# A decoder block on one core: early reloads, a regrouped Toeplitz product, and PSUM dealt from one pool

## The chip, the cores and the metric

The kernel runs on one core of a Trainium2 chip. Its time is the device time of one execution in microseconds. The median of three runs is given; lower is better. TensorE (PE) does the matrix products; VectorE (DVE), ScalarE (ACT) and GpSimd (POOL) do the elementwise work; SyncE (SP) mostly issues DMAs, of which POOL also issues some.

## The reference

One layer, 512 positions, width 1024, all float32. With h = RMSNorm(x), one projection h @ w_in gives eight pieces: u_s, z_s, q, k, v, z_a, r_s, r_a. Then

```
y_s = s5_branch(u_s, ...)                        # diagonal complex state space, 64 groups of 16 channels, 64 states
y_s = (y_s * silu(z_s)) @ w_ssm_out
q, k = rope(rms_norm(q)), rope(rms_norm(k))      # 3 dilated groups x 8 heads x 64
y_a = dilated_attention(q, k, v)
y_a = (y_a * silu(z_a)) @ w_attn_out
m   = sigmoid(r_s) * y_s + sigmoid(r_a) * y_a
out = x + m @ w_o

s5_branch(u):   h[l] = ab * h[l-1] + bb @ u[l]   # complex, per group
                y[l] = Re(c @ h[l]) + d_skip * u[l]
                g = gelu(y);  return g * sigmoid(g @ w_glu)
```

## The kernel before, in words

**Projections.** Each float32 operand is split into two rounded halves, hi and lo, and a product becomes three matmuls (hi·hi, lo·hi, hi·lo; `mm3`, all recorded at L63; transposes at L67). `hT_hi` and `hT_lo` hold h transposed. `cm_unit` takes one 1024x128 piece of weights and issues 24 matmuls of 512 columns into a PSUM tile `pj`. Weights come in the order of a list, two pieces ahead: `load_w` sends the DMA on SP's queue (L189) into one of two buffers `w_raw`, ACT rounds it to `w_hi` (L108), and DVE subtracts to get `w_lo` (L110). A third load into `w_raw` can only start when both readers of the first are done.

**S5 branch.** Positions are taken in chunks of eight. There are eight units j, each of eight groups (128 channels).

- `u_unit(j)`: a projection, copied by ACT into `uT` (L286), written by SP to a DRAM buffer `ud[j]` (L287). Later it is read back in another layout by `load_u` (L266), into a tile `Uj` from the pool of small buffers `t2k`.
- `w_unit(j)`: coefficients of chunk input to chunk state, by `coef` (L277 to L279: a product, a second product, a sum, each 128x512, twice per unit), then eight transposes into two PSUM tiles `wps`, copied by ACT into `W` (L299). The first product and the sum run on DVE; the second product runs on the engine that `coef` is given.
- `x_unit(j)`: `load_u`, then 16 matmuls into `xps`, copied by ACT into the chunk states `Xs`.
- A scan over chunks on DVE, L614 to L665, reads and writes `Xs`.
- `ca_unit(j)`: loads C, turns it by matmuls with an identity into `cps`, negates parts into `p3`, and runs `coef` (each op 128x576) for the coefficients `ca` of chunk state to output.
- `m_unit(j)`: 16 matmuls `kps` with `ca` give the in-chunk (Toeplitz) products, 16 rows by 128 columns each. A product reads one of two halves of the rows of the array (h) and writes one of four column groups (a = a0 + h). ACT copies them to `kt` (four copies, L734), POOL adds the skip term (L735), and POOL sends eight DMAs (L739) that lay `kt` out as a block Toeplitz matrix `M`, in one of three buffers.
- `y_unit(j)`: 16 matmuls with `M` and the reloaded u, then 32 with `ca` and `Xs`, into two tiles `yps`, copied to `ysb` (L765). `g_unit(j)` transposes it into `yT`, and ACT (L776) and DVE apply gelu and split it into `gT`.

Between these steps the program places other projections, called fillers (gates z_a and z_s, values, r_s, r_a), to keep PE busy. After the branch come w_glu, w_ssm_out, then attention for four pairs of heads (`qtp`: q and k turned and split at L873 on ACT and L874 on DVE; `sps`: scores; `ptp` and `ot`: probabilities turned, and values), w_attn_out and w_o.

**PSUM.** Eight banks: a pool `ps_p` of three buffers for `pj` and a pool `ps_g` of five for the rest. Behind the S5 branch these are closed and replaced by pools of four, three and one (`ot`). Each pool hands out a buffer as one comes free.

**Order.** Each engine has its own list of instructions, in an order fixed when the program is built: a scheduler of the framework moves instructions by its own estimates of when their operands and buffers are ready. So a change in one place moves instructions on all engines.

Of the kernel before, what the change touches and what calls it, by code (L numbers as in the profile page):

```python
# [11 lines left out]
F32 = mybir.dt.float32  # L12
# [8 lines left out]
P = 128  # L21
D = 1024
S = 512
# [29 lines left out]
def tile_hybrid_block(ctx: ExitStack, tc: tile.TileContext, x, positions, norm_w, w_in, lam_re, lam_im,  # L53
# [24 lines left out]
    tmp = ctx.enter_context(tc.tile_pool(name="tmp", bufs=6))  # L78
    sml = ctx.enter_context(tc.tile_pool(name="sml", bufs=2))
    dram = ctx.enter_context(tc.tile_pool(name="dram", bufs=1, space=DRAM))  # L80
    ps_first = ExitStack()
    ps_p = ps_first.enter_context(tc.tile_pool(name="ps_p", bufs=3, space=PSUM))
    ps_g = ps_first.enter_context(tc.tile_pool(name="ps_g", bufs=5, space=PSUM))

    scr_t = big.tile([P, 4096], F32, name="scr", tag="s4")
    scr_o = [0]
# [11 lines left out]
        return v if dtype == F32 else v.bitcast(dtype)  # L98

    def bank(name):  # L100
        return ps_g.tile([P, 512], F32, name=name, tag="g")

    def t2k(name, dtype=F32):
        return tmp.tile([P, 512], dtype, name=name, tag="t2k")
# [89 lines left out]

    def cm_unit(rh, rl, kts=KT):
        hi, lo = get_w()
        ps = ps_p.tile([P, 512], F32, name="pj", tag="pj")
        for k in range(kts):
            mm3(ps, hi[:, k], lo[:, k], rh[:, k], rl[:, k], k == 0, k == kts - 1)
        return ps  # L200
# [62 lines left out]
    def load_u(j, Uj=None):  # L263
        if Uj is None:
            Uj = t2k("Uj")
        sp.dma_start(Uj, ud[j].rearrange("q g s c -> s q g c"))  # L266
        return Uj.rearrange("p (g c) -> p g c", g=8)
# [21 lines left out]
    def w_unit(j):  # L289
        ba = ab[j % 2][:, 0:8 * T * Q].rearrange("p (a g k q) -> p a g k q", a=2, g=4, k=T)  # L290
        p4 = slice(4 * j, 4 * j + 4)
        for a in range(2):
            coef(ba[:, a], 4 * j, BB[:, 1 + a, p4], BB[:, a, p4], 1, T + 1, ab[2][:, 512 * a:], pool)
        W = big.tile([P, 8, P], F32, name="W", tag=("s6a", "s6b")[j % 2])
        for h in range(2):
            ps = bank("wps")
            for g in range(4):
                pe.transpose(ps[:, g * P:(g + 1) * P], ba[:, h, g].rearrange("p k q -> p (k q)"), ident)
            act.copy(W[:, 4 * h:4 * h + 4].rearrange("p g n -> p (g n)"), ps)  # L299
        return W  # L300

    def x_unit(j, W):
        Uj = load_u(j)
        ps = bank("xps")
        pv = ps.rearrange("p (a g c) -> p a g c", a=2, g=4)
        for g in range(4):
            for a in range(2):
                for h in range(2):
                    pe.matmul(pv[64 * h:64 * h + 64, a, g, :], W[:, 4 * a + g, 64 * h:64 * h + 64], Uj[:, 2 * g + h, :],
                              start=True, stop=True, skip_group_check=True)  # L310
        for a in range(2):
            act.copy(Xsv[:, a, 4 * j:4 * j + 4, NJ:C], pv[:, a, :, 0:C - NJ])
            act.copy(Xsv[:, a, 4 * j:4 * j + 4, 0:NJ], pv[:, a, :, C - NJ:C])

    first = [(get_w(), ps_p.tile([P, 512], F32, name="pj", tag="pj")) for _ in range(3)]
    for h in range(2):
        for (hi, lo), ps in first:
            for k in range(KT):
# [144 lines left out]

    for j in range(3, 8):
        u_unit(j)
        wx(*((), (), (0,), (1,), (2, 3))[j - 3])


    sza = cst.tile([P, NP, S], F32, name="sza")
    gd = dram.tile([2, KT, P, S], F32, name="gd")  # L470

    def gate_tile():
# [95 lines left out]

    def tok_granule():

        pss = [ps_p.tile([P, 512], F32, name="pj", tag="pj") for _ in range(2)]
        for kh in range(2):
            hi, lo = get_w()
            for b in range(2):
                for rr in range(2):
                    r = 2 * b + rr
                    o = pss[b][:, rr * 256:(rr + 1) * 256]
                    for k in range(4):
                        kk = 4 * kh + k
                        mm3(o, hT_hi[:, kk, r * P:(r + 1) * P], hT_lo[:, kk, r * P:(r + 1) * P],  # L580
                            hi[:, k], lo[:, k], kh == 0 and k == 0 and rr == 0, kh == 1 and k == 3)
        return pss
# [109 lines left out]
    def ca_unit(j):  # L692

        cn = sml.tile([P, P], F32, name="cn")
        rows = slice(j * P, (j + 1) * P)
        sp.dma_start(cn[:, 0:64], c_re[0].rearrange("g p n -> (g p) n")[rows])
        sp.dma_start(cn[:, 64:128], c_im[0].rearrange("g p n -> (g p) n")[rows])
        ps = bank("cps")
        for i in range(3):
            a = i % 2  # L700
            for h in range(2):
                pe.matmul(ps[64 * h:64 * h + 64, 64 * i:64 * i + 64], cn[:, 64 * a:64 * a + 64], idp[:, h],
                          start=True, stop=True, skip_group_check=True)

        p3 = sml.tile([P, 3, 4, Q], F32, name="p3")
        p3f = p3.rearrange("p a g q -> p (a g q)")
        act.copy(p3f[:, 0:64], ps[:, 0:64])
        act.activation(p3f[:, 64:192], ps[:, 64:192], AF.Copy, scale=-1.0)
        ca = ab[j % 3].rearrange("p (a g k q) -> p a g k q", a=2, g=4, k=9)
        for a in range(2):  # L710
            coef(ca[:, a], 4 * j, p3[:, a], p3[:, a + 1], 0, 9, abt[:, 3 * nca:], dve)

        dg = sml.tile([Q, 8, Q], F32, name="dg")
        sp.dma_start(dg.rearrange("q g p -> q (g p)"), d_skip[0:1, rows].to_broadcast([Q, P]))
        pool.tensor_tensor(dg, dg, ident[0:Q, 0:Q].unsqueeze(1).broadcast_to([Q, 8, Q]), op=ALU.mult)
        return ca, dg

    def m_unit(j, ca, dg):

        kt = big.tile([Q, 8, T, Q], F32, name="kt", tag=("s7a", "s7b")[j % 2])  # L720
        ps = bank("kps")

        for a0 in (0, 2):
            for b in range(2):
                for c in range(2):
                    for h in range(2):
                        a, m = a0 + h, 2 * b + a0 // 2
                        sl = slice(64 * h, 64 * h + 64)
                        pe.matmul(ps[32 * a:32 * a + Q, b * P:(b + 1) * P], BB[sl, 1 + c, 4 * j + m, :],
                                  ca[sl, c, m, 1:9, :], start=c == 0, stop=c == 1, skip_group_check=True,  # L730
                                  tile_position=(64 * h, 32 * a))
        kv = kt.rearrange("q (b a) k p -> q a b (k p)", a=4)
        for a in range(4):
            act.copy(kv[:, a], ps[32 * a:32 * a + Q, 0:2 * P].rearrange("q (b m) -> q b m", b=2))  # L734
        pool.tensor_tensor(kt[:, :, T - 1, :], kt[:, :, T - 1, :], dg, op=ALU.add)  # L735

        M = Mb[j % 3]
        for t in range(T):
            pool.dma_start(M[Q * t:Q * t + Q, :, 0:P - Q * t], kt[:, :, t:].rearrange("q g k p -> q g (k p)"))  # L739
        return M  # L740
# [75 lines left out]

    def wide_granule(th, tl, mid=None):

        pss = [ps_p.tile([P, 512], F32, name="pj", tag="pj") for _ in range(NB)]
        for kq in range(4):  # L820
            if mid:
                mid(kq)
            hi, lo = get_w()
            for r in range(NB):
                for k in range(2):
                    kk = 2 * kq + k
                    mm3(pss[r], th[:, kk, r * P:(r + 1) * P], tl[:, kk, r * P:(r + 1) * P], hi[:, k], lo[:, k],
                        kk == 0, kk == KT - 1)
        return pss
# [156 lines left out]
        return Pt  # L986

    def values(hp, Pt, V):
        ot = ps_o.tile([P, 512], F32, name="ot", tag="o")
        ov = ot.rearrange("d (r b j) -> d b r j", r=4, b=4)  # L990
        pend = []

# [44 lines left out]
        split(aT[:, 0, hp], aT[:, 1, hp], at, lo_eng=pool)  # L1037


    ps_first.close()  # L1040
    ps_p = ctx.enter_context(tc.tile_pool(name="ps_p2", bufs=4, space=PSUM))
    ps_g = ctx.enter_context(tc.tile_pool(name="ps_g2", bufs=3, space=PSUM))
    ps_o = ctx.enter_context(tc.tile_pool(name="ps_o", bufs=1, space=PSUM))
    yT_hi = big.tile([P, KT, S], F32R, name="yT_hi", tag="s1")
    yT_lo = big.tile([P, KT, S], F32R, name="yT_lo", tag="s2")
    for c in range(KT):
# [81 lines left out]
    for cc in range(KT // 2):  # L1128
        hi, lo = get_w()
        for c2 in range(2):  # L1130
            c = 2 * cc + c2
            if c in rals:
                th = rals[c]
            else:
                th = t2k("ral")
                sp.dma_start(th, rad[c])
            ps = ps_p.tile([P, 512], F32, name="pj", tag="pj")
            for k in range(NP):
                mm3(ps, hi[:, k, c2 * P:(c2 + 1) * P], lo[:, k, c2 * P:(c2 + 1) * P], aT[:, 0, k], aT[:, 1, k],
                    k == 0, k == NP - 1)  # L1140
            dve.scalar_tensor_tensor(th, th, 1.0, ps, op0=ALU.add, op1=ALU.mult)
            dve.tensor_tensor(th, th, m1[:, c], op=ALU.add)
            split(mT_hi[:, c], mT_lo[:, c], th, scale=0.5)
# [38 lines left out]
```

## Time and profile before

| what | value |
|---|---|
| three runs | 727.94, 728.95, 730.92 us, median 728.95 |
| profiled execution | 727.79 us, of which the profile's span is 726.0 and 1.8 lie around it |
| PE busy | 691.6 us, 95% of the span, 4821 matmuls |
| DVE, ACT, POOL busy | 455.4, 314.6, 190.9 us |
| mean granted clock of PE | 0.991 |
| S5 branch: first W coefficients to the last gelu | about 57 to 282 us of the span |

A busy time adds up one engine's instructions; what the program waits for is read from the idle time of PE and from what ended it. Times inside the trace are in us from the start of the span. A matmul of 512 columns is listed with 0.39 us, but the next one starts before its end, so prices of matmuls are taken from the starts of a row of them.

### The profile page before, as it was taken

How to read it: one execution, taken by the hardware profiler on the slowest of the kernel's cores; microseconds unless marked ns; L12 is line 12 of the kernel's file. 1: busy time of each engine (PE TensorE's matmuls, PEld its weight loads, DVE VectorE, ACT ScalarE, POOL GpSimd, SP SyncE). 2: the span in 40 equal slices, each digit the busy share in tenths (PEclk: the TensorE clock that was granted, in tenths of full speed). 3: DMA queues.
4: the chain of work that ended last, by engine and by line, in shares of the span. 5: the costliest groups of instructions: out<-in, count | busy, mean ns of one | idle time of the engine just before them, and what ended most of it. 6: DMA issues, size and time to landing. Idle time of an engine off the chain costs nothing.

```text
span 726.0 us, 12680 instructions
## 1 busy us (share of the span) xinstructions
PE 691.6 (95%) x4821; PEld 574.3 (79%) x4821; DVE 455.4 (63%) x912; ACT 314.6 (43%) x631; POOL 190.9 (26%) x346
## 2 busy tenths in 40 slices
PE   2799799999999999999999999999989998999997
PEld 2787687788978887888889888788868877888886
DVE  6859663999956645764325659755764667464832
ACT  6433453332326465442144456537253725443320
POOL 3426540140205343450000326121601160230000
PEclk9999899999999999999999999999999999999999
DMA  8433652564546544455333432322312231327441
GB/s 206 106 99 93 169 135 79 142 159 132 122 131 147 127 105 138 129 166 185 95 102 94 131 88 63 84 59 59 115 32 60 62 112 30 116 74 249 130 145 58
DMA packets 137213, 82.14 MB, mean 113 GB/s; under 512 B 32696, under 2 KB 125632, under 8 KB 137024
## 3 DMA queue, kind: packets, MB, share of 16 engines
q1 hardware_dynamic: 135088, 78.96, 38.0%
q0 software_dynamic: 2048, 2.36, 2.6%
q8 instruction: 38, 0.62, 0.4%
q14 instruction: 23, 0.19, 0.1%
q10 hardware_dynamic: 16, 0.00, 0.0%
HBM read 68.46 MB, written 10.49 MB: 109 GB/s over the span
## 4 chain that ended last, share of the span: by engine, by line
PE 89%; DVE 3%; ACT 2%; SPq 2%; DMA 2%; issue 1%; ACTq 0%
PE pj L63 73%; PE sps L63 3%; PE yps L63 3%; PE ot L63 2%; PE ptp L67 2%; PE kps L63 2%; PE xps L63 1%; DMA Uj<-ud 1%; PE qtp L67 1%; SPq L443 1%; PE wps L67 1%; DVE w_lo L110 1%; DMA w_raw<-in_w_in_dram 1%; ACT qkp L873 1%; SPq L219 1%; ACT w_hi L108 1%
## 5 line engine op out<-in xcount | busy, mean ns | idle before, releaser
L108 ACT ACTIVATE w_hi<-w_raw 128x1024 fp32r<-128x1024 f32 x100 | 106.1, 1062 | 231.8 <-PE pj L63 197.4
L110 DVE TENSOR_TENSOR w_lo<-w_raw,w_hi 128x1024 fp32r<-128x1024 f32 x98 | 124.5, 1271 | 106.5 <-ACT w_hi L108 106.0
L63 PE MATMUL pj<-hT_lo,w_hi 128*128 128x512 f32 (+1 forms) x344 | 130.9, 381 | 3.6 <-DVE hT_lo L252 3.6
L63 PE MATMUL pj<-hT_hi,w_hi 128*128 128x512 f32 (+1 forms) x344 | 130.8, 383 | 2.0 <-ACT V L905 1.4
L63 PE MATMUL pj<-hT_hi,w_lo 128*128 128x512 f32 (+1 forms) x344 | 130.7, 381 | 1.6 <-DVE w_lo L110 1.6
L63 PE MATMUL pj<-w_hi,hT_hi 128*128 128x512 f32 (+1 forms) x288 | 105.6, 368 | 0.0
L63 PE MATMUL pj<-w_lo,hT_hi 128*128 128x512 f32 (+1 forms) x288 | 105.6, 367 | 0.0
L63 PE MATMUL pj<-w_hi,hT_lo 128*128 128x512 f32 (+1 forms) x288 | 105.2, 368 | 0.0
L63 PEld LDWEIGHTS pj<-hT_lo,w_hi 128*128 128x128 f32 x344 | 65.5, 190 | 15.6 <-DVE hT_lo L252 4.5
L63 PEld LDWEIGHTS pj<-hT_hi,w_lo 128*128 128x128 f32 x344 | 65.5, 190 | 14.4 <-DVE w_lo L110 2.6
L63 PEld LDWEIGHTS pj<-hT_hi,w_hi 128*128 128x128 f32 x344 | 65.1, 191 | 14.5 <-ACT V L905 2.1
L63 PEld LDWEIGHTS pj<-w_hi,hT_lo 128*128 128x128 f32 x288 | 54.3, 189 | 8.8
L63 PEld LDWEIGHTS pj<-w_hi,hT_hi 128*128 128x128 f32 x288 | 54.3, 189 | 8.8 <-issue 0.2
L63 PEld LDWEIGHTS pj<-w_lo,hT_hi 128*128 128x128 f32 x288 | 54.4, 189 | 8.6
L931 ACT ACTIVATE Pt<-Pt,st 128x256 f32<-128x256 f32 (+1 forms) x64 | 31.0, 492 | 18.4 <-DVE st L929 18.4
L852 POOL TENSOR_TENSOR rt<-qraw,tC 128x256 f32<-128x256 f32 x12 | 14.1, 1175 | 86.8 <-DVE qraw L846 86.5
L735 POOL TENSOR_TENSOR kt<-kt,dg 16x128 f32<-16x128 f32 x8 | 4.8, 597 | 120.7 <-ACT kt L734 116.2
L739 POOL DMA_DIRECT2D dd<-kt x64 | 33.7, 535 | 2.4 <-POOL kt L735 2.4
L874 DVE SCALAR_TENSOR_TENSOR qkp<-qtp,wcol,qkp 128x512 fp32r<-128x512 f32 (+1 forms) x32 | 23.0, 746 | 12.7 <-ACT qkp L873 12.7
L961 POOL COPY sw<-st 32x4 f32<-32x4 f32 x64 | 12.0, 187 | 71.4 <-ACT Pt L931 68.6
L873 ACT ACTIVATE qkp<-qtp,wcol 128x512 fp32r<-128x512 f32 (+1 forms) x32 | 20.8, 685 | 15.2 <-PE qtp L67 10.0
L278 POOL TENSOR_TENSOR ab<-dd,AT 128x512 f32<-128x512 f32 x16 | 22.0, 1385 | 14.1 <-DVE ab L279 14.1
(263 smaller groups left out, 1289.0 us busy)
## 6 DMA issues: line engine op xcount, KB each, us to landing
w_raw<-in_w_in_dram SPq DMA_DIRECT2D x40, 512.0 KB
w_raw<-in_w_in_dram SPq DMA_DIRECT2D x112, 128.0 KB
w_raw<-in_w_glu_dram SPq DMA_DIRECT2D x8, 512.0 KB
w_raw<-in_w_ssm_out_dram SPq DMA_DIRECT2D x8, 512.0 KB
w_raw<-in_w_o_dram SPq DMA_DIRECT2D x8, 512.0 KB
x_all<-in_x_dram SPq DMA_DIRECT2D x4, 512.0 KB
ud<-uT SPq DMA_DIRECT2D x8, 256.0 KB
Uj<-ud SPq DMA_DIRECT2D x8, 256.0 KB
```

Source lines behind the costliest of these rows:

```text
L63: last[0] = nc.tensor.matmul(*a, **k)
L67: last[0] = nc.tensor.transpose(*a, **k)
L108: act.activation(hi, src, AF.Copy, scale=scale)
L110: e.tensor_tensor(lo, src, hi.bitcast(F32), op=ALU.subtract)
L219: sp.dma_start(x_t[r], xv[r])
L278: eng.tensor_tensor(tv, a2.unsqueeze(2).broadcast_to(sh), ai, op=ALU.mult)
L739: pool.dma_start(M[Q * t:Q * t + Q, :, 0:P - Q * t], kt[:, :, t:].rearrange("q g k p -> q g (k p)"))
L852: pool.tensor_tensor(t1, rh[:, :, :, 0:16], cv.broadcast_to([P, NB * 2, 2, 16]), op=ALU.mult)
L873: act.activation(hi, ps[sl], AF.Copy, scale=w)
L874: dve.scalar_tensor_tensor(lo, ps[sl], w, hi.bitcast(F32), op0=ALU.mult, op1=ALU.subtract)
L931: act.activation(o, o, AF.Exp, bias=nm, scale=-1.0, accum_out=st[:, kind, 1, h, b:b + 1])
L961: pool.tensor_copy(sw[32 * r:32 * r + 32, :, :, b], st[32 * b:32 * b + 32, 1, :, :, r])
```

## The change

Five edits.

1. After the fourth u unit is issued, the reloads of units 0, 1 and 2 are issued at once, and that of unit 3 after the fifth. They go into `sza`, a tile for a gate that is filled later, and no longer into buffers of `t2k` inside `x_unit`.
2. `coef` in `w_unit` is given DVE instead of POOL, so the 16 second products of 128x512 move.
3. The loops of `m_unit` are turned round: consecutive pairs of products now go to column groups 0, 1 and 2, 3 in turn, where before all products of groups 0 and 1 came first.
4. C is turned by four matmuls instead of six; the third part is copied from the first.
5. One PSUM pool of eight tags with one buffer each. The program deals the tags in a fixed rotation, in the order of the program text: three for `pj` and five for the rest, later four and three, with one kept for `ot`.

```diff
-    ps_first = ExitStack()
-    ps_p = ps_first.enter_context(tc.tile_pool(name="ps_p", bufs=3, space=PSUM))
-    ps_g = ps_first.enter_context(tc.tile_pool(name="ps_g", bufs=5, space=PSUM))
+    psum = ctx.enter_context(tc.tile_pool(name="psum", bufs=1, space=PSUM))
+    deal = {"p": [0, 1, 2], "g": [3, 4, 5, 6, 7]}
+    dealt = {"p": 0, "g": 0}
+
+    def ps_tile(kind, name):
+        tags = deal[kind]
+        dealt[kind] += 1
+        return psum.tile([P, 512], F32, name=name, tag="b%d" % tags[dealt[kind] % len(tags)])
...
-            coef(ba[:, a], 4 * j, BB[:, 1 + a, p4], BB[:, a, p4], 1, T + 1, ab[2][:, 512 * a:], pool)
+            coef(ba[:, a], 4 * j, BB[:, 1 + a, p4], BB[:, a, p4], 1, T + 1, ab[2][:, 512 * a:], dve)
...
+    sza = cst.tile([P, NP, S], F32, name="sza")
+    early = {}
...
-        Uj = load_u(j)
+        Uj = early.pop(j) if j in early else load_u(j)
...
     for j in range(3, 8):
         u_unit(j)
+        for i in {3: (0, 1, 2), 4: (3,)}.get(j, ()):
+            early[i] = load_u(i, sza[:, i])
         wx(*((), (), (0,), (1,), (2, 3))[j - 3])
...
-        for i in range(3):
-            a = i % 2
+        for i in range(2):
+            a = 1 - i
...
-        act.copy(p3f[:, 0:64], ps[:, 0:64])
-        act.activation(p3f[:, 64:192], ps[:, 64:192], AF.Copy, scale=-1.0)
+        act.copy(p3f[:, 0:64], ps[:, 64:128])
+        act.activation(p3f[:, 64:192], ps[:, 0:128], AF.Copy, scale=-1.0)
...
-        for a0 in (0, 2):
-            for b in range(2):
-                for c in range(2):
+        for b in range(2):
+            for c in range(2):
+                for a0 in (0, 2):
...
-        ot = ps_o.tile([P, 512], F32, name="ot", tag="o")
+        ot = psum.tile([P, 512], F32, name="ot", tag="b7")
...
-    ps_first.close()
-    ps_p = ctx.enter_context(tc.tile_pool(name="ps_p2", bufs=4, space=PSUM))
-    ps_g = ctx.enter_context(tc.tile_pool(name="ps_g2", bufs=3, space=PSUM))
-    ps_o = ctx.enter_context(tc.tile_pool(name="ps_o", bufs=1, space=PSUM))
+    deal.update(p=[0, 1, 2, 3], g=[4, 5, 6])
```

The lists of the engines before and after show where instructions moved. First SP's list, from the write of the third u unit on (each row is a DMA; `ud<-uT` is a write to DRAM, `w_raw` a load of weights). Before:

```order
L287 DMA ud_215<-uT_388 8x16x512
L189 DMA w_raw_530<-in_w_in_dram 128x8x128
L189 DMA w_raw_564<-in_w_in_dram 128x8x128
L189 DMA w_raw_598<-in_w_in_dram 128x8x128
L287 DMA ud_215<-uT_561 8x16x512
L189 DMA w_raw_651<-in_w_in_dram 128x8x128
L287 DMA ud_215<-uT_595 8x16x512
L189 DMA w_raw_727<-in_w_in_dram 128x8x128
L287 DMA ud_215<-uT_629 8x16x512
L189 DMA w_raw_934<-in_w_in_dram 128x8x128
L266 DMA Uj_704<-ud_215 128x8x64
```

The same place after the change:

```order
L295 DMA ud_212<-uT_386 8x16x512
L197 DMA w_raw_528<-in_w_in_dram 128x8x128
L274 DMA sza_214<-ud_212 128x8x64 x3
L197 DMA w_raw_565<-in_w_in_dram 128x8x128
L197 DMA w_raw_600<-in_w_in_dram 128x8x128
L295 DMA ud_212<-uT_559 8x16x512
L274 DMA sza_214<-ud_212 128x8x64
L197 DMA w_raw_653<-in_w_in_dram 128x8x128
L295 DMA ud_212<-uT_596 8x16x512
L197 DMA w_raw_727<-in_w_in_dram 128x8x128
```

Three reloads now stand one weight load behind the third write, ahead of two weight loads, and the fourth stands behind the fourth write. Before, the first reload stood behind six weight loads and three more writes.

Next PE's list where x unit 0 stands. Before, it comes 28 projection matmuls behind the second group of eight `wps`:

```order
L63 MATMUL pj<-hT_lo,w_hi 128x512
L63 MATMUL pj<-hT_hi,w_lo 128x512
L63 MATMUL pj<-hT_hi,w_hi 128x512
L63 MATMUL xps<-Uj,W 64x64 x16
L67 MATMUL wps<-ident,ab 128x128 x8
```

After the change:

```order
L63 MATMUL pj<-hT_lo,w_hi 128x512
L63 MATMUL pj<-hT_hi,w_lo 128x512
L67 MATMUL wps<-ident,ab 128x128 x8
L63 MATMUL xps<-sza,W 64x64 x16
L63 MATMUL pj<-hT_hi,w_hi 128x512
```

X unit 0 now stands straight behind the second group of `wps`.

Last PE's list for the third pair of heads, where q and k are turned. Before:

```order
L67 MATMUL qtp<-ident,qraw 128x4x32 x8
L67 MATMUL qtp<-ident,qraw 128x128 x8
L67 MATMUL ptp<-ident,Pt 128x128 x10
L63 MATMUL ot<-ptb,V 64x4x32
L67 MATMUL ptp<-ident,Pt 128x128 x4
L63 MATMUL ot<-ptb,V 64x4x32 x5
```

After the change, up to the first values:

```order
L67 MATMUL qtp<-ident,qraw 128x4x32 x8
L63 MATMUL pj<-w_hi,hT_lo 128x512
L63 MATMUL pj<-w_hi,hT_hi 128x512
L63 MATMUL pj<-w_lo,hT_hi 128x512
L67 MATMUL qtp<-ident,qraw 128x128 x4
L63 MATMUL pj<-w_hi,hT_lo 128x512
L63 MATMUL pj<-w_hi,hT_hi 128x512
L63 MATMUL pj<-w_lo,hT_hi 128x512
L63 MATMUL pj<-w_hi,hT_lo 128x512
L67 MATMUL qtp<-ident,qraw 128x128 x4
L67 MATMUL ptp<-ident,Pt 128x128 x10
L63 MATMUL ot<-ptb,V 64x4x32 x6
```

Seven projection matmuls of 512 columns now stand between the turns of q and k; the fourth pair's list changes in the same way.

More of the change, by code (lines that the diff above doesn't have):

```diff
@@ L100, in bank, with pj_tile @@
     def bank(name):
-        return ps_g.tile([P, 512], F32, name=name, tag="g")
+        return ps_tile("g", name)
+    def pj_tile():
+        return ps_tile("p", "pj")
     def t2k(name, dtype=F32):
@@ L196, in cm_unit @@
         hi, lo = get_w()
-        ps = ps_p.tile([P, 512], F32, name="pj", tag="pj")
+        ps = pj_tile()
         for k in range(kts):
@@ L313, in x_unit @@
             act.copy(Xsv[:, a, 4 * j:4 * j + 4, 0:NJ], pv[:, a, :, C - NJ:C])
-    first = [(get_w(), ps_p.tile([P, 512], F32, name="pj", tag="pj")) for _ in range(3)]
+    first = [(get_w(), pj_tile()) for _ in range(3)]
     for h in range(2):
@@ L465, in tile_hybrid_block @@
         u_unit(j)
+        for i in {3: (0, 1, 2), 4: (3,)}.get(j, ()):
+            early[i] = load_u(i, sza[:, i])
         wx(*((), (), (0,), (1,), (2, 3))[j - 3])
-    sza = cst.tile([P, NP, S], F32, name="sza")
     gd = dram.tile([2, KT, P, S], F32, name="gd")
@@ L569, in tok_granule @@
     def tok_granule():
-        pss = [ps_p.tile([P, 512], F32, name="pj", tag="pj") for _ in range(2)]
+        pss = [pj_tile() for _ in range(2)]
         for kh in range(2):
@@ L817, in wide_granule @@
     def wide_granule(th, tl, mid=None):
-        pss = [ps_p.tile([P, 512], F32, name="pj", tag="pj") for _ in range(NB)]
+        pss = [pj_tile() for _ in range(NB)]
         for kq in range(4):
@@ L1136, in tile_hybrid_block @@
                 sp.dma_start(th, rad[c])
-            ps = ps_p.tile([P, 512], F32, name="pj", tag="pj")
+            ps = pj_tile()
             for k in range(NP):
```

## The prediction, made before the changed kernel was run

> **What bounds the kernel.** I read the page's first part and its chain, then what ended PE's idle time, then the stages in windows, and then the rows around the places that the change touches.
>
> ```profile
> span 726.0 us, 12680 instructions
> PE 691.6 (95%) x4821; PEld 574.3 (79%) x4821; DVE 455.4 (63%) x912; ACT 314.6 (43%) x631; POOL 190.9 (26%) x346
> PE 89%; DVE 3%; ACT 2%; SPq 2%; DMA 2%; issue 1%; ACTq 0%
> ```
>
> PE is busy for 691.6 of 726.0 us and makes up 89% of the chain. So only three things pay: PE's idle 34.4 us, PE running at a lower clock, and products that can run side by side. PE's waits (us in all, times, longest) show which idle time the change can reach:
>
> ```profile
> PE hps L67 <- DVE x_all L240: 10.1, 1, 10.1
> PE xps L63 <- DMA Uj<-ud: 4.5, 1, 4.5
> PE qtp L67 <- DVE qkp L874: 3.5, 2, 1.8
> PE pj L63 <- DVE w_lo L110: 1.6, 2, 0.9
> PE pj L63 <- ACT V L905: 1.4, 3, 0.5
> PE pj L63 <- ACT gs L776: 1.0, 1, 1.0
> PE wps L67 <- DVE ab L279: 0.6, 1, 0.6
> PE yT L67 <- ACT ysb L765: 0.2, 1, 0.2
> ```
>
> The first row is the start, which stays. The rows in reach are the reload of u, the weight split, the W coefficients, the last gelu and the turning of q and k. The stages, with PE's granted clock and the DMA share and GB/s at the end:
>
> ```profile
> 57.27:91.10 33.83, 27.85 (x150) 22.39 (x151) 27.36 (x42) 13.18 (x20) 19.82 (x16) 0.90 0.55 140
> 77.44:80.85 3.41, 0.82 (x4) 0.35 (x2) 2.46 (x3) 0.67 (x2) 2.78 (x3) 1.00 0.59 160
> 80.85:87.68 6.83, 4.90 (x43) 4.58 (x44) 3.85 (x5) 3.96 (x8) 2.07 (x2) 0.50 0.69 166
> 528.00:531.41 3.41, 1.77 (x12) 1.30 (x13) 3.14 (x5) 2.90 (x8) 0.00 (x0) 1.00 0.44 126
> 531.41:534.82 3.41, 3.41 (x20) 2.42 (x18) 2.02 (x4) 1.27 (x2) 0.00 (x0) 0.50 0.10 28
> 598.90:602.30 3.40, 1.90 (x13) 1.43 (x14) 3.12 (x6) 2.83 (x9) 0.00 (x0) 1.00 0.53 154
> ```
>
> The columns are the busy time of PE, PE's weight loads, DVE, ACT and POOL. The W stage (57.27 to 91.10) has 6.0 us of PE idle. In two places a stretch in which PE was busy for 0.82 or 1.77 of 3.41 us is followed by half clock; one with 1.90 of 3.40 is not. So a wait of about 1.7 us or more can be paid twice. [...]
>
> **Early reloads and coefficients on DVE: −5.0 us.**
>
> ```profile
> 76.73 0.39 PE L63 MATMUL pj<-hT_lo,w_hi 128*128 128x512 f32 x1
> 77.87 0.39 PE L63 MATMUL pj<-hT_hi,w_hi 128*128 128x512 f32 x1
> 74.81 7.83 DMA Uj<-ud
> 91.10 1.08 PE xps L63 x32
> 92.18 1.02 PE wps L67 x8
> 42.17 3.33 SPq L287 DMA_DIRECT2D ud<-uT  x3
> 65.71 0.37 SPq L189 DMA_DIRECT2D w_raw<-in_w_in_dram  x1
> ```
>
> Five steps of projection take 77.87 − 76.73 = 1.14 us, 0.228 each. The W stage's 150 records, less 24 `wps`, 32 of an x unit and a few small ones, leave 91 of them (20.7 us); with 24 `wps` (8 in 1.02: 3.1) and one x unit (1.08): 24.9 of 33.8 us. So 8.9 us are lost: 6.0 idle and 2.9 at half clock.
>
> The reload was issued at 74.81 and took 7.83, so x unit 0 waited 4.5 us. After the change it is issued behind the third write, whose issues end at 45.50 (42.17 + 3.33). If write and reload each take 7.83 it lands by 61.2; PE reaches x unit 0 at about 70.5 (70.7 less the 0.2 of a shorter walk below). The wait goes, and the half clock that followed it too. On SP's queue the three reloads stand ahead of the weight loads for the seventh and eighth u unit; at worst these come 7.8 us late, about 61, and DVE takes up the seventh only at 63. That costs nothing unless the reloads take over 10 us. x units 1 and 2 come earlier in PE's list in the same way.
>
> What is late next is DVE, and behind it ACT:
>
> ```profile
> 57.14 2.69 DVE L277 TENSOR_TENSOR ab<-dd,AT 128x512 f32<-128x512 f32 x4
> 59.33 2.49 POOL L278 TENSOR_TENSOR ab<-dd,AT 128x512 f32<-128x512 f32 x2
> 59.75 1.04 DVE L621 TENSOR_TENSOR scn<-A 128x32 f32<-128x32 f32 x1
> 62.40 1.28 DVE L279 TENSOR_TENSOR ab<-ab 128x512 f32<-128x512 f32 x2
> 63.60 2.08 DVE L110 TENSOR_TENSOR w_lo<-w_raw,w_hi 128x1024 fp32r<-128x1024 f32 x1
> 73.15 1.22 DVE L110 TENSOR_TENSOR w_lo<-w_raw,w_hi 128x1024 fp32r<-128x1024 f32 x1
> 71.26 1.06 ACT L108 ACTIVATE w_hi<-w_raw 128x1024 fp32r<-128x1024 f32 x1 [8.17 <-DMA w_raw<-in_w_in_dram]
> 72.22 1.07 ACT L286 COPY uT<-pj 128x512 f32<-128x512 f32 x1
> 73.07 1.13 ACT L299 COPY W<-wps 128x512 f32<-128x512 f32 x2
> ```
>
> A product of 128x512 takes 1.25 us on POOL (2.49 / 2) and about 0.6 on DVE (1.28 / 2). The same split took 2.08 us beside POOL's product and 1.22 with POOL out of the way: half of what DVE takes over it gets back. DVE's walk: four L277 to 59.75, two second products 1.2, scan tables about 0.9, two sums 1.2: 63.05, the moment at which PE has the first `wps` today. The split after it ends near 64.2 instead of 65.68. So the two small waits (0.6 and 0.9) become one of about 0.8. DVE has 27.36 us of work in 33.83; the 16 products add 10 us over the some 45 us of this stage and the next, which fits.
>
> The new wait: two ACT copies of W's first unit stand behind `w_hi` of the ninth weight tile. Its load can go when DVE ends the split at 64.2, lands 5.55 us later (today 65.71 to 71.26), then comes 0.96 of `w_hi`, about 0.9 of `uT` and 1.13 of W: about 72.8, where PE stands at 70.5: 2.3 us, and with half a chance of a window at half clock (1.7 us) 0.85 more. New losses 0.8 + 2.3 + 0.85 = 3.9 against 8.9. Between −9 (no new wait) and −1 (the wait as long as today's, with the dip).
>
> **Toeplitz order: −3.6 us; C turned once: −0.9.**
>
> ```profile
> 183.22 1.51 PE L63 MATMUL kps<-ab,dd 64*16 64x128 f32 x32
> 183.22:183.66 0.44, 0.44 (x8) 0.41 (x10) 0.00 (x0) 1.00 1.05 318
> 183.68:184.04 0.36, 0.36 (x20) 0.35 (x16) 0.00 (x0) 1.00 1.11 337
> 244.13 0.57 PE L63 MATMUL cps<-ident,cn 128*64 128x64 f32 x12
> ```
>
> For 0.44 us only column groups 0 and 1 work (8 records); then the products of groups 2 and 3 run beside the last of the first two and 20 records go in 0.36. With the groups dealt in turn, the overlap starts at once: a unit of 1.44 us becomes about 0.99, 0.45 × 8 units = 3.6. [...] C: four records fewer at 2 per 58 ns, 0.117 × 8.
>
> **PSUM and what it moves: −3.4 us in sum.** The last gelu (1.0 + 0.2 of wait): three filler units now stand between unit 7's turn and w_glu, some 15 us, −1.2. Attention: the third and fourth pair wait 1.8 and 1.7 us for a turned bank; seven projections now stand there (1.6 us), −1.2 each. The first of these waits lies in the window at 528 with 1.77 busy, and with 1.6 more the half clock behind it goes, −1.7. Against that, a fixed rotation hands out a bank in program order where before any free one was taken: +0.9, between 0 and the 1.8 of one such wait, the middle. Sum −3.2. The y stage: +1.0. Units come with fewer fillers between them, and M has a long chain:
>
> ```profile
> 229.18 1.29 PE L63 MATMUL kps<-ab,dd 64*16 64x128 f32 x28
> 232.89 4.20 POOL L739 DMA_DIRECT2D dd<-kt  x8 [0.30 <-POOL kt L735]
> dd<-kt POOLq DMA_DIRECT2D x8, 64.0 KB, 3.6
> ```
>
> From the end of `kps` (230.4) to the last landing is 6.7 to the last issue and 2.3 to 3.6 more, 9 to 10 us. In the changed list I count (with these prices) 11.6 us of PE between unit 3's products and its use, and 13.9, 16, 17 and 16 for the later units. So it just fits: nothing by this, up to +4 if the chain grows by half; I take a quarter of that.
>
> **The sum.** −5.0 − 3.6 − 0.9 − 1.2 − 3.2 + 1.0 = −12.9. From the profiled execution, 727.79, that is 714.9. The median of the runs, 728.95, stands 1.16 above it: 716.0.
>
> **Rivals.**
>
> 1. The reload's wait turns into another one: the W copies wait on ACT behind a late weight tile for as long as today, with the window at half clock. For: DVE is at 81% of the W stage and gets 10 us more. Against: the load's 5.55 us is shown and ends before today's reload. The gain there is 1 instead of 5: 720.
> 2. The fixed rotation binds in attention: a bank still held while others are free. For: three banks for scores, turned q and turned probabilities, each wait up to 1.8 us in today's rows. Then +2.5 instead of −3.2: 721.7.
> 3. Products on the same half of the rows don't overlap: 16 × 0.11 us (today's first 8 records, four products, take 0.44) = 1.76 a unit instead of 1.44, +2.5 instead of −3.6: 722.
> 4. The other side: M's chain is the new bound. It is paid in the y stage at units 3 to 7. At 18 us, twice today's, waits of 6.4, 4.1, 2, 1 and 2 make 15.5 instead of 1.0, so 730.5 or so, with a dip of clock 731.5. It decides from about 17.5 us on. For: eight DMAs of 64 KB on one queue. Against: nothing is added to that chain, and POOL loses work.
> 5. All goes well, x stage −9 and no new waits in the y stage: 710.
>
> **Chances.** Forecast 0.62, rivals in order 0.17, 0.09, 0.04, 0.04 and 0.04. The forecast's own range is 712 to 719.5 (x stage −9 to −1.5). The range from 710 to 723 leaves out rival 4 and the tails of the others. A measurement of this kernel can tell about 0.5%, 3.6 us. Faster than that 0.90, within it 0.06, slower 0.04 (rival 4).
>
> **What would show it.** Right: `xps` waits for no DMA; full clock from 77 to 91; `kps` x32 in about 1.0 us in the chain; `cps` x8; no wait on `gs`; qtp's waits under 1 us; span about 713. A new row "xps <- ACT W" of 2 to 3 us is expected; over 4 means rival 1. `kps` at 1.5 or more means rival 3; rows `yps <- DMA dd` mean rival 4; rows of `ptp`, `sps` or `qtp` waiting on ACT or DVE beyond today's mean rival 2. The forecast is wrong altogether if DVE, with ten more microseconds in a stage that it already fills to 81%, hands out weights late: `pj <- DVE w_lo` above 3 us.

## The result, and the profile after

The changed kernel takes 723.22 us (median of six runs, 721.68 to 723.72) against 729.18 for the kernel before; the ratio is 0.9923 (95% interval 0.9902 to 0.9943). It is faster by 6.0 us. The forecast was 716.0 with a range of 710 to 723: the sign is right, the size is half, and the time lies just outside the range.

The profiled execution took 722.95 us. Its page (span, busy times, chain):

```profile
span 721.2 us, 12599 instructions
PE 689.3 (96%) x4789; PEld 571.6 (79%) x4789; DVE 460.8 (64%) x928; ACT 314.8 (44%) x631; POOL 179.8 (25%) x330
PE 87%; ACT 4%; DMA 4%; SPq 2%; DVE 2%; issue 0%; ACTq 0%
```

PE has 31.9 us of idle time where it had 34.4. DMA and ACT, each 2% of the chain before, are now 4% each. PE's waits say where:

```profile
PE ptp L67 <- ACT ptb L1039: 3.5, 6, 0.8
PE xps L63 <- ACT W L307: 3.1, 1, 3.1
PE pj L63 <- DVE w_lo L118: 1.6, 3, 0.8
PE pj L63 <- ACT w_hi L116: 1.3, 2, 0.9
```

The wait of `xps` on the reload, those on the last gelu and those of `qtp` are gone. A wait of 3.1 us on W's copies and six waits, 3.5 us in all, on `ptb` (the probabilities, turned and copied by ACT) have come. To see where the span changed I cut both traces at the same events. The view of a tile gives its first and last start; here `wps`, `xps` and `qtp` of before:

```profile
L67 PE MATMUL wps<-ident,ab x64: 270/273/476, 63.1 to 116.2; 128*128 128x128 f32 x64
L63 PE MATMUL xps<-Uj,W x256: 222/222/366, 82.8 to 122.4; 128*64 128x64 f32 x128
L67 PE MATMUL qtp<-ident,qraw x96: 270/272/328, 405.7 to 623.6; 128*128 128x128 f32 x96
```

and of the changed kernel:

```profile
L67 PE MATMUL wps<-ident,ab x64: 270/272/328, 65.5 to 117.4; 128*128 128x128 f32 x64
L63 PE MATMUL xps<-Uj,W x128: 222/222/271, 106.7 to 123.9; 128*64 128x64 f32 x128
L67 PE MATMUL qtp<-ident,qraw x96: 270/272/273, 403.2 to 618.2; 128*128 128x128 f32 x96
```

| stretch of PE's list | before | after | change | forecast |
|---|---|---|---|---|
| start to first `wps` | 63.1 | 65.5 | +2.4 | 0 |
| first `wps` to last `xps` | 59.3 | 58.4 | −0.9 | −5.0 |
| last `xps` to first `qtp` (Toeplitz, C, y stage, gelu) | 283.3 | 279.3 | −4.0 | −4.7 |
| first `qtp` to the end | 320.3 | 318.0 | −2.3 | −3.2 |

Apart from the 32 records of C that the change saves, each stretch holds the same PE records in both traces, within six. The last two rows came nearly as forecast. The missing time is in the first two; the second of them is where the forecast put the early reloads and the move of the coefficients.

### The profile page after: what moved, and what is told of

It reads as the page before. It is cut to its first block, busy times and chain, and to the rows that moved or that the text cites. A ratio compares the mean times of both kernels' runs of the same rounds, so it can differ in the third digit from the quotient of the medians.

```text
span 721.2 us, 12599 instructions
## 1 busy us (share of the span) xinstructions
PE 689.3 (96%) x4789; PEld 571.6 (79%) x4789; DVE 460.8 (64%) x928; ACT 314.8 (44%) x631; POOL 179.8 (25%) x330
## 4 chain that ended last, share of the span: by engine, by line
PE 87%; ACT 4%; DMA 4%; SPq 2%; DVE 2%; issue 0%; ACTq 0%
PE pj L63 72%; DMA w_raw<-in_w_in_dram 4%; PE yps L63 3%; PE sps L63 3%; PE ot L63 2%; PE ptp L67 2%; PE xps L63 1%; PE kps L63 1%; ACT w_hi L116 1%; PE qtp L67 1%; SPq L454 1%; PE wps L67 1%; ACT qkp L885 1%; PE yT L67 1%; SPq L227 1%; ACT ptb L1039 1%
## 5 line engine op out<-in xcount | busy, mean ns | idle before, releaser
L63 PE MATMUL pj<-hT_hi,w_hi 128*128 128x512 f32 (+1 forms) x344 | 132.9, 389 | 2.7 <-ACT V L917 1.4
L747 POOL TENSOR_TENSOR kt<-kt,dg 16x128 f32<-16x128 f32 x8 | 12.0, 1505 | 92.0 <-ACT kt L746 86.0
L990 POOL COPY sfb<-sd 32x2 f32<-32x2 f32 x64 | 18.0, 282 | 27.9 <-DVE sd L986 25.1
```

Source lines behind the costliest of these rows:

```text
L63: last[0] = nc.tensor.matmul(*a, **k)
L990: pool.tensor_copy(fb[32 * b:32 * b + 32, :, r], d[32 * r:32 * r + 32, 1, :, b])
```

## The experiments

Each kernel was timed beside the kernel before, on the same chip. Not all rows come from one chip, so rows are compared best by their ratios. "Changed" is the kernel of this case.

| kernel | us, median | ratio to before, 95% interval |
|---|---|---|
| changed | 723.22 | 0.9923 (0.9902 to 0.9943) |
| before + early reloads alone | 727.91 | 0.9996 (0.9979 to 1.0013) |
| before + coefficients on DVE alone | 722.54 | 0.9927 (0.9900 to 0.9954) |
| before + Toeplitz order alone | 723.23 | 0.9925 (0.9906 to 0.9944) |
| before + PSUM dealing alone | 726.12 | 0.9973 (0.9958 to 0.9988) |
| changed, coefficients back on POOL | 722.08 | 0.9919 (0.9899 to 0.9939) |
| changed, no early reloads | 716.73 | 0.9852 (0.9826 to 0.9878) |
| changed, early reloads written later | 722.43 | 0.9924 (0.9902 to 0.9946) |
| changed, early reloads from POOL's queue | 720.51 | 0.9890 (0.9854 to 0.9927) |
| changed, early reloads for nobody, 256-byte rows | 725.17 | 0.9962 (0.9946 to 0.9978) |
| changed, early reloads for nobody, 2 KB rows | 725.81 | 0.9966 (0.9953 to 0.9979) |
| changed, one early reload | 715.57 | 0.9832 (0.9815 to 0.9848) |
| changed, no early reloads, old PSUM pools | 719.72 | 0.9896 (0.9875 to 0.9917) |

### What the W stage waits for now

The trace of the changed kernel gave the first theory. SP's queue:

```profile
44.56 3.33 SPq L295 DMA_DIRECT2D ud<-uT  x3
47.99 0.57 SPq L197 DMA_DIRECT2D w_raw<-in_w_in_dram  x1
48.69 10.38 SPq L274 DMA_DIRECT2D sza<-ud  x3
59.17 2.93 SPq L197 DMA_DIRECT2D w_raw<-in_w_in_dram  x2
```

and, on ACT, the weight tiles and the first copies of W:

```profile
57.71 1.06 ACT L116 ACTIVATE w_hi<-w_raw 128x1024 fp32r<-128x1024 f32 x1 [5.93 <-DMA w_raw<-in_w_in_dram]
65.92 1.06 ACT L116 ACTIVATE w_hi<-w_raw 128x1024 fp32r<-128x1024 f32 x1 [5.63 <-DMA w_raw<-in_w_in_dram]
75.07 1.06 ACT L116 ACTIVATE w_hi<-w_raw 128x1024 fp32r<-128x1024 f32 x1 [5.50 <-DMA w_raw<-in_w_in_dram]
76.88 1.11 ACT L307 COPY W<-wps 128x512 f32<-128x512 f32 x2
```

The three reloads take 10.4 us to issue. The weight load behind them, of the second tile in these rows, goes at 59.17 and its tile is taken up at 65.92. The later tiles are late with it, and W's copies stand behind the split of the fourth, taken up at 75.07. The wait ends at 77.57, and a half clock follows:

```profile
78.94:82.35 3.41, 3.41 (x14) 2.65 (x10) 3.41 (x6) 2.83 (x8) 0.00 (x0) 0.50 0.72 194
```

Four kernels were run on this. The first lets the program ask for the reloads later.

```diff
-        for i in {3: (0, 1, 2), 4: (3,)}.get(j, ()):
+        for i in {4: (0,), 5: (1,), 6: (2,), 7: (3,)}.get(j, ()):
```

> The changed kernel, but the reloads of units 0 to 3 are written one behind each of the u units 4 to 7, so one weight load now stands between the first reload and the next two. Theory A (three reloads in a row hold SP's queue for 10.4 us, so the next weight tile is issued at 59.2, and ACT reaches the first copies of W 3.1 us late): the next weight tile is issued near 52, the wait of xps on the W copies falls from 3.1 to under 1.5 us, the half clock after it goes, and the time falls by 2 to 5 us against the changed kernel, to about 719.5. Theory B (DVE, which got the coefficients, is what is late in that stage): W copies and the wait stay, 723 within 1 us. Theory C (the stage lost only by the phase of the clock window at 34 to 41 us): also 723, with the time differing only as that dip does.

Measured: 722.43, no change. The scheduler still drew all reloads forward; only one weight load moved ahead of two of them. It was issued 7.2 us behind the third write (at 49.35, the write at 42.20) instead of 14.6, and its tile was taken up at 59.22, and yet `xps` waited 4.1 us for W. So Theory A's forecast failed, but SP's queue still held a weight load. These are SP's rows further on, of the fourth early reload and of the load of the fourth tile:

```profile
66.40 0.58 SPq L274 DMA_DIRECT2D sza<-ud  x1
67.08 1.00 SPq L197 DMA_DIRECT2D w_raw<-in_w_in_dram  x1
```

That reload reads what the fourth u unit wrote. SP stood 4.5 us until the write had landed, and the weight load stood behind it, although its buffer was free at 63.56, when DVE ended the split of the second tile. In the kernel with one early reload (below) the second tile is taken up at nearly the same time, 59.10, and the same load goes out as soon as its buffer is free:

```profile
63.52 0.37 SPq L197 DMA_DIRECT2D w_raw<-in_w_in_dram  x1
```

The fourth tile is taken up at 73.41 here and at 68.65 there, W is copied at 75.22 and 70.47, and the times are 722.43 and 715.57. In the changed kernel the same queueing costs this load 1.1 us (free at 68.24, issued at 69.36); the rest of its lateness follows the second tile's. The second kernel takes the reloads off SP's queue.

```diff
+            early[i] = load_u(i, sza[:, i], pool)   # pool.dma_start instead of sp.dma_start
```

> The changed kernel, but the four early reloads are issued from POOL's queue, so SP's queue holds only the weight loads and the writes there. Theory A: the weight tiles come as before the change (the next one issued by 52), xps waits under 1.5 us for the W copies, 719 to 720. Theory B: as the changed kernel, 723 within 1 us. If the transfers themselves (3 x 256 KB beside the weights) and not the queue hold the weights back, the weight tile is issued early but lands as late as now, near 65, and the time stays at 723.

Measured: 720.51 (715.37 to 724.17), between the two forecasts; the runs spread over both, so the trace has to decide. SP's row for three weight loads, the piece of the chain of waits behind it, and the reloads (issues, KB each, median us to landing):

```profile
45.13 12.91 SPq L197 DMA_DIRECT2D w_raw<-in_w_in_dram  x3
45.79 19.26 DMA w_raw<-in_w_in_dram
sza<-ud POOLq DMA_DIRECT2D x3, 256.0 KB, 13.6
```

The load of the second tile went out at 45.79, ahead of all four reloads, and landed 19.3 us later, at 65.05. Without early reloads (next kernel) the three loads start at 46.60 and that tile is taken up at 57.49, at most 10.9 us later. So the weight load took 8.4 us longer or more (19.3 less 10.9), although the reloads stood in another queue. The third leaves the early reloads out.

```diff
-        for i in {3: (0, 1, 2), 4: (3,)}.get(j, ()):
-            early[i] = load_u(i, sza[:, i])
```

> The changed kernel without the early reloads (x units reload into small buffers as before the change); the other four parts stay. Theory A: the early reloads earned little on balance, since the wait on the reload (4.5 us) was traded for late weights and the wait on W: 723 to 725. Theory B: the early reloads earned their 4.5 us and the clock dip behind it and DVE ate it: 728 to 730.

Measured: 716.73, better than either theory had it: the early reloads cost 6.5 us by the medians and 5.2 by the ratios. Its waits and rows of SP, ACT and the chain:

```profile
PE xps L63 <- DMA Uj<-ud: 1.2, 1, 1.2
46.60 11.98 SPq L197 DMA_DIRECT2D w_raw<-in_w_in_dram  x3
57.49 1.06 ACT L116 ACTIVATE w_hi<-w_raw 128x1024 fp32r<-128x1024 f32 x1
69.65 1.11 ACT L307 COPY W<-wps 128x512 f32<-128x512 f32 x2
73.86 5.57 DMA Uj<-ud
```

The second weight tile is split at 57.49 instead of 65.92 and W is copied at 69.65 instead of 76.88. The reload goes out at 73.86, still late, but lands in 5.57 us instead of 7.83, and x unit 0 waits 1.2 us instead of 4.5. No window in this stage falls to half clock (the mean clock of this execution is 0.998, of the changed kernel's 0.993): from the first `wps` (64.8) to the last `xps` (117.7) it takes 52.9 us, against 59.3 before and 58.4 in the changed kernel. The fourth gives the early reloads alone to the kernel before.

```diff
+        for i in {3: (0, 1, 2), 4: (3,)}.get(j, ()):
+            early[i] = load_u(i, sza[:, i])
...
-        Uj = load_u(j)
+        Uj = early.pop(j) if j in early else load_u(j)
```

> The kernel before with the early reloads alone (coefficients stay on POOL, old Toeplitz order, old C, old PSUM pools). Theory A: the reload's wait goes, but weights are late by the same 10 us of queue: 726 to 729, near no change. Theory B: 722 to 724, the full 5 us, since DVE isn't loaded here.

Measured: 727.91 against 727.74, ratio 0.9996: nothing that shows. The reload's wait of 4.5 us is gone there, and waits on late weights take 2.6 of it back (1.2 us on W, 2.5 on `w_lo` after 1.6, 1.1 on `w_hi` after 0.6). In its trace the stage is still 2.5 us shorter (56.8 for 59.3); the interval of the times leaves room for a gain of 1.5. Theory A's number was right here, and Theory B was wrong: alone the reloads earn little or nothing, and beside the other parts they cost 5 to 6.5 us.

### The other parts one by one

```diff
-            coef(..., pool)
+            coef(..., dve)
```

> The kernel before with the W coefficients on DVE alone. Theory D (the move to DVE is what pays in the W stage, because DVE and POOL no longer slow each other; the early reloads then take it back by holding up the weight transfers): the W stage ends some 4.7 us earlier than before, as without early reloads, 722 to 725. Theory E (the gain without early reloads comes from the PSUM dealing, which also moves instructions there): no change, 727 to 729.

Measured: 722.54, ratio 0.9927. Theory D holds: moving the coefficients is what earns the 5 us that the forecast gave to both edits. In its trace the first `wps` to the last `xps` take 53.8 us, 5.5 less than before. Its rows of DVE, beside the 2.08 and 1.04 us of before, and of x unit 0 show why:

```profile
62.44 1.21 DVE L110 TENSOR_TENSOR w_lo<-w_raw,w_hi 128x1024 fp32r<-128x1024 f32 x1
61.53 0.18 DVE L621 TENSOR_TENSOR scn<-A 128x32 f32<-128x32 f32 x1
78.98 1.15 PE L63 MATMUL xps<-Uj,W 128*64 128x64 f32 x32 [0.71 <-DMA Uj<-ud]
```

With POOL out of the way the split ends at 63.65 instead of 65.68, the weight loads go out at 63.68, 67.63 and 73.06 instead of 65.71, 71.39 and 74.40, and x unit 0 starts at 78.98 instead of 82.78, behind the reload that follows them on SP's queue. DVE's list changed too: the split now stands ahead of two sums. How much the shorter operations give and how much the new order was not measured apart. Why DVE is slower beside POOL is not shown either; the traces have only the lengths: 0.9 us more on a 1.2 us operation, beside two POOL products that took 3.44 us together.

The reverse, with the early reloads in place:

```diff
-            coef(..., dve)
+            coef(..., pool)
```

> The changed kernel with the W coefficients back on POOL. Theory D: with the early reloads in place the weights are late either way, so DVE's relief is worth little: 721 to 724, as the changed kernel. If the DVE move pays its some 5 us in any case: 727 to 729.

Measured: 722.08, the same as the changed kernel. So the two edits of this stage do not add: with the early reloads the weights are late whichever engine forms the products.

```diff
-        for a0 in (0, 2):
-            for b in range(2):
-                for c in range(2):
+        for b in range(2):
+            for c in range(2):
+                for a0 in (0, 2):
```

> The kernel before with the Toeplitz products dealt round four column groups alone. If the overlap is real and nothing gives it back: 3.5 us, about 724.5. If the saving is lost to M's chain, which then starts as late as before and is used sooner: 727 to 728.

Measured: 723.23, ratio 0.9925, 4.6 us by the medians. One unit's products in this kernel's PE timeline:

```profile
133.67 0.41 PE L63 MATMUL kps<-ab,dd 64*16 64x128 f32 x8
138.81 0.84 PE L63 MATMUL kps<-ab,dd 64*16 64x128 f32 x24
```

24 records now take 0.84 us where 28 took 1.29. Summed from the starts of all 256 records, `kps` fell from 12.3 to 8.8 us, by 3.5. No wait on M came.

The edit in words, not in code:

```diff
-    ps_p, ps_g, ps_o: pools whose buffers go to whoever asks
+    psum: eight tags, dealt in a fixed rotation
```

> The kernel before with the PSUM pool dealt in fixed rotation alone. Theory D: the last gelu's wait goes (1.2 us), the waits for turned q and k go (3.5) with the half clock behind the first (1.7) but new waits on ptb come (3): about 3 us, 724 to 726; the W stage as before. Theory E: 722 or less, with the W stage 4 to 5 us shorter too.

Measured: 726.12, ratio 0.9973: a small gain, and the W stage keeps its 4.0 us wait on the reload, so Theory E is out. Its waits hold the trade that the changed kernel shows too:

```profile
PE xps L63 <- DMA Uj<-ud: 4.0, 1, 4.0
PE ptp L67 <- ACT ptb L1035: 3.5, 6, 0.8
```

3.5 us of waits of `qtp` went and 3.5 of `ptp` came; what is left is the half clock at 531 us, which is gone, and the last gelu's wait. The products with C in the y stage rose by 1.2 us (from 8.7 to 9.9, summed from their starts). Unbroken rows of 64 records take 1.09 us in both traces; the rise is in the rows of the first units, which now run together or are broken up by other products. The order of the Toeplitz products alone leaves the sum at 8.8.

### Which property of the early reloads costs

Two kernels keep the early transfers but give them to nobody: the x units reload late, as in the version of 716.7 us.

```diff
-        Uj = early.pop(j) if j in early else load_u(j)
+        Uj = load_u(j)
```

> The changed kernel in which the x units reload u late, as before the change, while the four early reloads stay where they are and fill sza for nobody: 4 x 256 KB of transfers in 256-byte packets more than the version without early reloads (716.7 us). Theory F (what costs is the transfers themselves, which share the DMA engines with the weight tiles): the weight tiles land as late as in the changed kernel, near 65, and the time is 721 to 725. Theory G (what costs is the moving of x unit 0 ahead in PE's list, to where W's copies are not ready): x unit 0 stands late again, so 716 to 718.

The second moves the same bytes in long rows.

```diff
-            early[i] = load_u(i, sza[:, i])
+            sp.dma_start(sza[:, i], ud[i].rearrange("q g s c -> g q (s c)"))
```

> As the kernel before in this call, with the same bytes at the same places of SP's queue, but read as they lie in DRAM, in rows of 2 KB: 128 packets per transfer for 1024. Theory F with packets: the packets cost, not the bytes; the weight tiles land nearly as without early reloads (by 60) and the time is 716 to 719. If the bytes cost, or four more entries on SP's queue: the same as the kernel with 256-byte packets, within 1 us.

Measured: 725.17 and 725.81, the same. Four transfers that nobody reads cost 8.4 and 9.1 us. Theory G is out: x unit 0 stands late again, and the time is long all the same. Theory F's forecast holds, though these two kernels do not part the transfers from SP's queue, which they also fill. SP's rows and the wait, first with 256-byte rows, then with 2 KB rows:

```profile
45.57 10.45 SPq L274 DMA_DIRECT2D sza<-ud  x3
56.11 3.40 SPq L197 DMA_DIRECT2D w_raw<-in_w_in_dram  x2
PE xps L63 <- DMA Uj<-ud: 6.1, 1, 6.1
```

```profile
46.97 7.47 SPq L478 DMA_DIRECT2D sza<-ud  x3
54.53 3.88 SPq L197 DMA_DIRECT2D w_raw<-in_w_in_dram  x2
PE xps L63 <- DMA Uj<-ud: 6.2, 1, 6.2
```

With an eighth of the packets the three issues take 7.5 us instead of 10.4, and the second tile is taken up 19.5 us behind the third write instead of 22.0 (without early reloads 14.3). So the packets cost something there, and the transfers themselves more. The kernel's time does not show it: the load of the fourth tile again stands behind the fourth reload: its buffer is free at 64.64 and it goes out at 69.11, where with small packets it was free at 65.78 and went at 66.91. So the reload that x unit 0 needs is as late. The finer theory, that the packets cost and not the bytes, failed; what the packets would cost in time without the fourth reload is not shown. The last pair asks for the best version.

```diff
-        for i in {3: (0, 1, 2), 4: (3,)}.get(j, ()):
+        for i in {5: (0,)}.get(j, ()):
```

> The changed kernel with only unit 0's reload early, the others late as before. Theory F: a third of the disturbance; the weight tile behind it is 2 to 3 us late, in a stage where the ACT takes up the next tile some 4 us after it lands, so little of it shows, and the 1.2 us that x unit 0 still waits for its reload without early loads go: 715.5 to 718. Theory G: x unit 0 is moved ahead in PE's list as in the changed kernel and waits 3 us for W's copies: 720 to 723.

Measured: 715.57, ratio 0.9832 (0.9815 to 0.9848), the fastest kernel of this study. ACT and PE there:

```profile
59.10 1.06 ACT L116 ACTIVATE w_hi<-w_raw 128x1024 fp32r<-128x1024 f32 x1 [2.18 <-DMA w_raw<-in_w_in_dram]
70.47 1.11 ACT L307 COPY W<-wps 128x512 f32<-128x512 f32 x2
71.68 1.15 PE L63 MATMUL xps<-sza,W 128*64 128x64 f32 x32
```

The second weight tile is taken up at 59.10, 1.6 us later than without any early reload and 6.8 us earlier than with all four. This reload's data was written long before, so nothing on SP's queue waits for it. W is copied in time, and x unit 0 stands ahead in PE's list as in the changed kernel and starts at 71.68 with no wait. Of the 1.2 us over the version without early reloads the medians show 1.16; their runs overlap, so only the gain over the changed kernel is certain.

The last edit, in words again:

```diff
-    psum: eight tags, dealt in a fixed rotation
+    ps_p, ps_g, ps_o as before, early reloads left out
```

> The changed kernel without the early reloads and with the PSUM pools of before. If the parts add (PSUM dealing alone gave 1.7 us): 718 to 719, against 716.7 with the dealing. If the dealing gives nothing here, 716 to 717.5.

Measured: 719.72 against 716.73 with the dealing: 3 us where 1.7 had been measured alone. Its trace has a wait that no other trace of this study has: a product of the y stage stands 1.8 us for M's DMAs (`yps` on `dd`). So M's chain, rival 4 of the forecast, is not far from setting a wait.

## Why the prediction was half right

**Right.** PE as the bound; the Toeplitz order (−3.6 forecast, −3.5 measured, rival 3 out); C (−0.9 forecast, −0.7 in the changed kernel's trace, where `cps` takes 3.2 us for 3.9; no run has it alone); the last gelu (−1.2, both waits are gone); the M chain, which set no wait in the changed kernel (rival 4 out there). The y stage was to lose 1.0, by waits. Its products took 1.2 us more, summed from their starts, and nothing waited, so the number came out by luck.

**Right in sum, wrong in its parts: attention.** Forecast −3.2, measured −2.3. The waits of `qtp` fell by 3.5 instead of 2.4 and the half clock went (a half clock shows in attention in four of the five traces with the old pools and in none of the nine with the new dealing; in those four, seven `ptp` records in a row take 1.26 to 1.74 us, in the fifth 0.98). But the waits of `ptp` took 3.1 more (3.5 on `ptb`), against 0.9 allowed for. That is rival 2's mechanism, at about a sixth of its price (0.9 of 5.7).

**Wrong: the W stage.** The step that failed is the one on SP's queue: the weight loads behind the reloads would come "at worst 7.8 us late, about 61", and "that costs nothing unless the reloads take over 10 us". They took 10.4 us to issue, and the tile was taken up at 65.92. The price of one reload, 7.83 us, was used for three at once, and what they cost a weight load of 512 KB in flight beside them, 8.4 us or more when POOL issued them, was priced at nothing. So was the fourth reload, which stood on SP's queue until its write had landed (4.5 us in the kernel that asks for the reloads later). The new losses were put at 3.9 us (a wait of 2.3 on W, 0.8 on the weights and half a chance of the half clock); the trace has 3.1 on W, 1.3 on the weights and the half clock whole, 1.7. So rival 1 came true with its place, its half clock and most of its wait (3.1 us on W's copies, for 4.5), but through the DMAs and not through DVE's load. Without the early reloads the time is 716.73, and the forecast was 716.0; that is luck in part, since the forecast had the 5 us of this stage from the reloads.

The second wrong step lumped two edits into one −5.0 and credited it to the reload. Measured apart, the coefficients earn 5.3 us and the reloads nothing that shows; together, in the stretch of the table, 0.9. I had called DVE's ten extra microseconds the danger of this stage; moving them there was its gain. (Rival 5's 710 is a slip: by its own terms it comes to 711.)

**Not foreseen: +2.4 us before the stage.** It lies ahead of the third write of u (issued at 44.56, at 42.17 before), where of the five edits only the PSUM dealing acts; the kernel with that alone has this write at 41.73. Three windows of the changed kernel's start:

```profile
31.15:34.56 3.41, 1.40 (x9) 1.18 (x9) 3.38 (x15) 2.20 (x7) 3.41 (x18) 1.00 0.00 0
34.56:37.97 3.41, 2.59 (x13) 2.34 (x12) 3.41 (x16) 0.95 (x2) 0.51 (x1) 0.50 0.00 0
37.97:41.39 3.42, 3.42 (x18) 3.42 (x18) 3.34 (x14) 0.00 (x0) 0.00 (x0) 0.50 0.00 0
```

Here two windows ran at half clock, in the profiled execution before only one (33.06 to 36.48, clock 0.50). The other traces go the same way. With no window at half clock between 31.15 and 41.39 the third write is issued at 41.4 to 42.2 (five traces), with one at 42.2 to 43.2 (six), with two at 43.6 to 44.6 (three: the changed kernel, and the kernels with the coefficients alone and with the Toeplitz order alone, whose starts are that of before). So I put this term down to the number of windows at half clock, two for one, and not to the change; why their number differs is not shown. There is only one trace of each kernel, so no run shows it changing between executions of one kernel.

## What to carry to other kernels

A transfer moved earlier is not free because its own wait disappears: look at what else is in flight at the new place and price the transfers there together, not one by one (the four early reloads cost 6.5 us here). When a wait ends with a DMA that was issued late, first ask what held up the loads ahead of it; here DVE, slowed beside POOL (2.08 us for 1.21), did, and mending that earned as much as the Toeplitz order, the best of the other edits (ratios 0.9927 and 0.9925). A reload that stood 4.5 us on SP's queue for its write held up the weight load behind it (free at 63.56, issued at 67.08), so place a DMA where its data has already landed. And when two edits aim at the same wait, give each its own term, since their gains did not add here: with the early reloads in place the time was 723.22 with the move of the coefficients and 722.08 without it.

## What the runs showed of the hardware

- Four transfers of 256 KB that nobody read cost 8 to 9 us of a 717 us kernel. In 128 packets of 2 KB each, three of them were issued in 7.5 us, and in 1024 packets of 256 bytes in 10.4 (the second trace has 4096 more packets under 512 bytes); the kernel's time did not change (725.81 and 725.17).
- A weight load of 512 KB that went out ahead of three reloads landed after 19.3 us, with the reloads in flight from another engine's queue; without them its tile was taken up at most 10.9 us after its issue.
- A reload whose data had not landed stood 4.5 us on SP's queue, and a weight load whose buffer was free at 63.56 went out behind it at 67.08.
- A DVE operation of 1.21 us took 2.08 beside POOL, and one of 0.18 took 1.04.
- Toeplitz products that return to the same half of the rows every second time, with the column groups dealt in turn, went 24 records in 0.84 us; with two column groups alone, 8 records took 0.44.
- One kernel's executions differ with the granted clock: the twelve of the early reloads alone go from 724.19 us at a mean clock of 0.997 to 729.38 at 0.991. By the difference of 0.006 alone I estimate 4.4 us (0.006 × 727) of these 5.2.
